# Attention's long steps before its short ones, and later tokens first through the output projection and the FFN, in a hybrid LRU / attention / RWKV-7 block

## The chip, the cores and the metric

The kernel runs on one core of a Trainium2 chip. The metric is device time of one execution in microseconds. Engines are named as in the profile: PE (TensorE, with PEld for its weight loads), DVE (VectorE), ACT (ScalarE), POOL (GpSimd), SP (SyncE, which issues nearly all transfers).

## The reference

One layer on 2048 tokens of width 1024, with 16 learned meta tokens in front (2064 rows). One input projection feeds three groups of heads; their outputs are concatenated to 1024 columns, projected, normalised and added; a gated FFN with a causal convolution of three taps follows.

```python
p = rms_norm(h, norm_mix_pre) @ w_in
oa = rg_lru_group(xa, ya, ...)                   # 256 columns, scan over tokens
ob = forgetting_attention_group(q, k, v, f, ...) # 512 columns, 8 heads of 64, causal
oc, _ = rwkv7_group(pc, ...)                     # 256 columns, scan over tokens
h = h + rms_norm(concat([oa, ob, oc]) @ w_out, norm_mix_post)
f = causal_dwconv(rms_norm(h, norm_ffn_pre) @ ffn_up, ffn_conv)   # 3 taps
gate, val = split(f)
h = h + rms_norm((gelu(gate) * val) @ ffn_down, norm_ffn_post)
# attention of one block of 128 queries, one head:
s = q @ k.T + (c[query] - c[key])   # c: running sum of log forget gates
o = softmax(where(key <= query, s, -inf)) @ v
```

Everything is float32. The kernel multiplies nearly all large products in three passes over high and low parts.

## The kernel before, in words

The framework plans the order of each engine's instructions itself, on a modelled timeline; what stands earlier in the program goes first where both could run. `tc.issue_after(ins)` puts what a block issues behind a given instruction on its engine. The stages, in the order of the program:

1. **Input projection** in three parts of the tokens (lines 158 to 281), with the recurrences beside it: `Beside.advance` (line 1842) steps the LRU blocks and the nine RWKV blocks (`Rwkv.block`, line 955) between column strips. The RWKV blocks follow each other through a state. Each has a triangular solve in which POOL (line 1101) and DVE (line 1102) take turns fifteen times. What is left of the recurrences when the projection ends is issued by `beside.finish()` (line 1958). The RWKV holds three PSUM banks (`ps_rw`, `ps_ae`), the projection five.
2. **Attention** (`Attn`, line 394). A step is one head and 512 queries, `b` of 0 to 3. It has `4b + 5` key tiles: 5 and 9 in a short step (b of 0, 1), 13 and 17 in a long one (b of 2, 3). `maxima` (line 485) multiplies queries with keys once to find each row's maximum; each piece goes to a PSUM bank (`mx`, line 448) that DVE reduces (line 512). `weights` (line 603) multiplies scores again (lines 635 and 636), takes exponentials on ACT (line 640), adds them up for the denominator, three of four on POOL and the rest on DVE (line 679), and multiplies with the values on PE (line 658). The maxima of a step are interleaved with the weights of the step two before it (`AHEAD`). After a step the denominator goes through DRAM and back (`total`, `invert`, `scale`), some ticks later. `run` (line 753) does the short steps of all eight heads, then the meta tokens, then the long steps. `mx` takes turns over two banks, or over three from the point `WIDE` on; the third one, `more`, is the RWKV's former `ps_ae`.
3. **Output projection** (`w_out_tile`, line 1421), 17 token tiles: tile 0 with two rows, tiles 1 to 16 with 128 rows each. A tile is 48 matmuls into two banks, then norm, residual and its row statistics. It reads 1024 rows of the concatenated heads (`scr["mix"]`), so it needs LRU, RWKV and all attention heads of its tokens. Its weights are loaded and split (line 144, 145) in memory that the RWKV gave back. Tiles 0 to 8 need only short attention steps, tiles 9 to 16 the long ones. Places 7 and 8 (`HELD`) are held behind the last but one attention step; from place 8 (`LATE`) on each tile is followed by an `ffn_norm` of the first FFN turn.
4. **FFN up** (`ffn_up`, line 1611) in three turns over the tokens (`SUPERS`), 684 tokens each, with 22 column pairs in each; the next turn's tokens are normalised by `between` during the one before.
5. **FFN down** (`Down`, line 1724) over pairs of token tiles, in two passes over the rows of `ffn_down`.

The order of the work around the change is written by hand in these few lines:

```python
for half, bs in enumerate(((0, 1), (2, 3))):   # 757
    if half: self.meta()
    for h in range(NH):
        self.wide = (half, h) >= WIDE          # 761, WIDE = (0, 5)
HELD = 7, 8                                    # 1821
for i, (f, rows) in enumerate(FFN_TILES):      # 1990
units = [(sup, j) for sup in range(SUPERS) for j in range(NFF)]   # 1618
```

Of the kernel before, what the change touches and what calls it, by code (L numbers as in the profile page):

```python
# [29 lines left out]
NFF = FF // P  # L30
# [363 lines left out]
class Attn:  # L394
# [358 lines left out]
    def run(self):  # L753


        ready = []
        for half, bs in enumerate(((0, 1), (2, 3))):
            if half:
                self.meta()
            for h in range(NH):  # L760
                self.wide = (half, h) >= WIDE
                keys = self.keys(h, 4 * bs[-1] + 5)
                for b in bs:
                    gen, total, out = self.maxima(h, b, keys), self.pieces(b), []

                    def fill(share, gen=gen, total=total, out=out):
                        while len(out) < min(total, share * total):
                            out.append(next(gen))

                    if len(ready) == self.AHEAD:  # L770
                        self.weights(*ready.pop(0), fill)
                    fill(1.0)
                    ready.append((h, b, keys, next(gen)))
        for step in ready:
            self.weights(*step, lambda share: None)
        self.flush()
        for _, _, f in self.later:
            f()
# [684 lines left out]
FFN_TILES = [(0, HALO)] + [(HALO + P * i, P) for i in range(SEQ // P)]  # L1463
# [3 lines left out]
SUPERS = 3  # L1467

# [33 lines left out]
def ffn_quarters(core, pool, sup):  # L1506

    t = pool.tile([P, len(QUARTERS), HK, FN], F32, tag="q", name=core.n("q"))
    q = {s: t[:, i] for i, s in enumerate(QUARTERS)}
    used = SEQ + HALO - FBLK * (2 * sup + 1)  # L1510
    if used < FN:
        for s in ("b0", "b1"):
            core.nc.gpsimd.memset(q[s][:, :, used:], 0.0)
    return q


def ffn_sums(core, q, after=nullcontext):

    q["t3"] = q["b0"]
    for k in range(HK):  # L1520
        for o, x, y in (("t1", "b0", "a0"), ("t2", "b1", "t1"), ("t3", "b1", "b0"), ("t4", "a1", "t2")):
            with after():
                core.nc.gpsimd.tensor_tensor(q[o][:, k], q[x][:, k], q[y][:, k], op=ALU.subtract)
            yield
# [86 lines left out]
def ffn_up(core, raws, ring, pool, banks, w_up, cw, scr, between, tokens):  # L1611

    nc = core.nc
    tt, stt = nc.vector.tensor_tensor, nc.vector.scalar_tensor_tensor
    turn = 0
    units = [(sup, j) for sup in range(SUPERS) for j in range(NFF)]
    ahead = UpWeights(core, raws, ring, w_up, scr, 0)
    ws = [ahead.operand(i) for i in range(7)]  # L1620
    xs = [tokens(0, i) for i in range(7)]

    def conv(src, u, j, n):
        y = pool.tile([P, FBLK], F32, tag="uy", name=core.n("uy"), bufs=UY)
        cc = u * NFF + j
        nc.scalar.activation(y[:, :n], src[:, 2 : n + 2], AF.Copy, scale=cw[:, 88 + cc : 89 + cc])  # L1626
        for i in (1, 0):
            stt(y[:, :n], src[:, i : n + i], cw[:, 44 * i + cc : 44 * i + cc + 1], y[:, :n], op0=ALU.mult, op1=ALU.add)  # L1628
        if u == 0:
            nc.scalar.activation(y[:, :n], y[:, :n], AF.Gelu_apprx_tanh)  # L1630
        return y

    def ending(g, v, j, b0, n):
        core.pooled = nc.gpsimd.tensor_tensor(v[:, :n], g[:, :n], v[:, :n], op=ALU.mult)  # L1634
        nc.sync.dma_start(scr["ff"][P * j : P * j + P, b0 : b0 + n], v[:, :n])

    for at, (sup, j) in enumerate(units):
        b0 = [FBLK * (2 * sup + i) for i in range(2)]
        n = [min(FBLK, SEQ - b) for b in b0]
        s = lambda tag: pool.tile([P, FN], F32, tag=tag, name=core.n(tag), bufs=1 if tag == "u2" else 2)[:]  # L1640
        between(sup, j)
        more = at + 1 < len(units)
        if more:
            ahead = UpWeights(core, raws, ring, w_up, scr, units[at + 1][1])
        ws_next, bank = [], {}
        turn ^= 1
        for i, (name, (_, _, at_)) in enumerate(PRODUCTS.items()):
            w, x = ws[i], xs[i]
            first = at_ not in bank
            if first:  # L1650
                bank[at_] = banks[turn].tile([P, 512], F32, tag="up", name=core.n("psu"))[:, :FN]
            ps = bank[at_]
            for k in range(HK):
                mm3(nc, ps, w[:, 0, k], w[:, 1, k], x[:, 0, k], x[:, 1, k], first and k == 0, k == HK - 1, not first)
            if j == NFF - 1 and more:
                xs[i] = tokens(sup + 1, i)
            if more:
                ws_next.append(ahead.operand(i))
            if name == "p1":
                ga = s("ga")  # L1660
                nc.scalar.activation(ga, ps, AF.Copy)
            elif name == "p5":
                vb = s("vb")
                nc.scalar.activation(vb, ps, AF.Copy)
            elif name == "p6":
                u2 = s("u2")
                nc.scalar.activation(u2, ps, AF.Copy)
            elif name == "p3":
                tt(ps, ps, u2, op=ALU.add)
                gb = conv(ps, 0, j, n[1])  # L1670
            elif name == "p7":
                tt(vb, ps, vb, op=ALU.add)
                vb = conv(vb, 1, j, n[1])
            elif name == "p2":
                tt(ps, ps, ga, op=ALU.add)
                ga = conv(ps, 0, j, n[0])
                ending(gb, vb, j, b0[1], n[1])
            else:
                va = conv(ps, 1, j, n[0])
                ending(ga, va, j, b0[0], n[0])  # L1680
        ws = ws_next
# [132 lines left out]
READY = 13  # L1814
PACE = 1.5

WIDE = (0, 5)

LATE = 8

HELD = 7, 8


class Beside:
# [54 lines left out]
def hybrid_block_kernel(ctx: ExitStack, tc: tile.TileContext, args, out):  # L1879
    a = {s: v[0] if s != "meta_tokens" else v for s, v in args.items()}  # L1880
    nc = tc.nc
    core = Core(tc, ctx)
    scr = scratch(tc, ctx, core)
# [4 lines left out]
    def run(gen):  # L1888
        for _ in gen:
            pass  # L1890
# [14 lines left out]
    with ExitStack() as p1:  # L1905
# [7 lines left out]
        with ExitStack() as p1a:  # L1913
# [5 lines left out]
            for part in range(3):  # L1919
# [6 lines left out]
                units = w_in_part(core, pools, ps_mm, a["w_in"], blocks, scr)  # L1926
# [42 lines left out]
    with ExitStack() as p3:  # L1969
# [11 lines left out]
        rs = {}  # L1981
        with p2:
            ps_wo.append(pool(p2, "ps_wo2", 1, space=PSUM, **right))
            banks = Banks(core, ps_wo)
            g_post = spread(pool(p2, "gpost", 1, **right), a["norm_mix_post"], "g_post")
            wp = pool(p2, "wp", 2, **right)
            w = w_out_load(core, wp, a["w_out"])
            todo = list(tiles[0])
            quarters = {0: ffn_quarters(core, qp, 0)}
            for i, (f, rows) in enumerate(FFN_TILES):  # L1990
                with tc.issue_after(at.steps[-2].ins) if i in HELD else nullcontext():
                    _, rs[i] = w_out_tile(
                        core, wp, banks, scr, w, x, meta, g_post, f + META - HALO, rows, rsv[:, 6 * i : 6 * i + 6]
                    )
                banks.wide = i >= LATE - 1
                if i >= LATE and todo:
                    q, f, rows = todo.pop(0)
                    ffn_norm(core, np_, ps_n, scr, f, rows, rs[q], g_fpre, quarters[0], 0)
                    if not todo:
                        run(ffn_sums(core, quarters[0]))  # L2000
        ps_f.append(pool(p3, "ps_f1", 3, space=PSUM, **early))
        uw += [pool(p3, "uw1", UWB, **early)] * UWB
        xo += [pool(p3, f"xo{i}", 1, **early) for i in range(3, XO)]
# [3 lines left out]

        def between(sup, j):

            sup += 1  # L2010
            if j == 1 and sup < SUPERS:
                quarters[sup] = ffn_quarters(core, qp, sup)
                todo[:] = tiles[sup]
            elif j == 1:
                kept = qp.tile([P, DOWN_KEPT, 2, 512], F32R, tag="q", name=core.n("qd"))
                down.extend(kept[:, i] for i in range(DOWN_KEPT))
            elif sup == SUPERS:
                if j == DOWN_FROM:
                    raw = lambda: tmp.tile([P, 512], F32, tag="uq", name=core.n("raw"))[:]
                    ws.append(down_operands(core, raw, lambda: down.pop(0), a["ffn_down"], scr, 0))  # L2020
            elif todo:
                q, f, rows = todo.pop(0)
                ffn_norm(core, np_, ps_n, scr, f, rows, rs[q], g_fpre, quarters[sup], sup)
                if not todo:
                    sums.append(ffn_sums(core, quarters[sup], lambda: tc.issue_after(core.pooled.ins)))
            else:
                for _ in range(2):
                    next(sums[-1], None)
# [78 lines left out]
```

## Time and profile before

| | us |
|---|---|
| median of 3 runs | 3129.16 (3125.92 to 3143.95) |
| the profiled execution | 3135.82 |
| its span in the profile, first to last instruction | 3134.1 |
| mean granted TensorE clock | 0.957 |
| PE busy | 2938.6 (94%) |
| DVE busy | 2218.7 (71%) |
| ACT busy | 1456.5 (46%) |
| POOL busy | 1320.1 (42%) |

A window is a stretch of the span in us from its start. Busy time is the union of an engine's instructions. PE's matmuls are pipelined and their ends are modelled, so 94% is not 94% of its peak. The granted clock is the share of full speed that TensorE had. A row of a view by line gives the count, the busy time, the mean duration in ns, and the idle time of the engine before those instructions with what ended it; a row of a view by window gives busy time and, in brackets, how many instructions fell into it.

### The profile page before, as it was taken

What the parts mean: (1) busy time and instruction counts of PE and PEld (TensorE: products, weight loads), DVE (VectorE), ACT (ScalarE), POOL (GpSimd) and SP (SyncE); (2) the same over time, 40 slices, a digit from 0 to 9 for tenths busy, and PEclk for the clock granted to TensorE, in tenths of its full rate; (3) what the DMA queues carried; (4) which work ended last, traced back from release to release, by engine and by line L of the source; (5) the groups of instructions that cost most, each with busy time, mean ns of one, the idle gap of its engine ahead of it and who ended that gap; (6) DMA issues with size and microseconds to landing.
All of it is one profiled execution on the core that took longest, in us unless ns stands there. A gap on an engine that the chain in (4) does not pass through costs nothing. (4 is left out here: it accounts for less than half of the span.)

```text
span 3134.1 us, 52572 instructions
## 1 busy us (share of the span) xinstructions
PE 2938.6 (94%) x18488; PEld 2504.0 (80%) x18488; DVE 2218.7 (71%) x4563; ACT 1456.5 (46%) x2716; POOL 1320.1 (42%) x1458
## 2 busy tenths in 40 slices
PE   6988899999988999999999899999999999999997
PEld 6978788888966665565557799999999999787776
DVE  6147665876678777877757787787778787647777
ACT  4133433444444434444543466666666665324332
POOL 3334334211013464645761235433533334547655
PEclk9989899999987888999999899999999999999999
DMA  6777766643453234535417365555555565435444
GB/s 195 224 237 224 219 197 217 204 129 109 116 128 83 72 84 108 147 96 134 97 43 232 123 188 168 165 172 167 165 166 165 168 189 163 170 105 165 148 155 141
DMA packets 493816, 484.10 MB, mean 154 GB/s; under 512 B 83200, under 2 KB 408010, under 8 KB 487904
## 3 DMA queue, kind: packets, MB, share of 16 engines
q1 hardware_dynamic: 493168, 480.36, 51.1%
q8 instruction: 145, 2.38, 0.3%
q14 instruction: 119, 0.97, 0.1%
q0 software_dynamic: 384, 0.39, 0.0%
HBM read 354.76 MB, written 125.87 MB: 153 GB/s over the span
## 5 line engine op out<-in xcount | busy, mean ns | idle before, releaser
L150 PE MATMUL psu<-xo,uw 128*128 128x344 f32 x1848 | 588.1, 323 | 7.8 <-DVE wx L1457 4.8
L151 PE MATMUL psu<-xo,uw 128*128 128x344 f32 x1848 | 593.2, 321 | 1.0 <-DVE xo L1529 1.0
L152 PE MATMUL psu<-xo,uw 128*128 128x344 f32 x1848 | 582.6, 320 | 0.0
L150 PE MATMUL psp<-xh,wh 128*128 128x384 f32 (+2 forms) x1152 | 384.5, 334 | 0.0
L152 PE MATMUL psp<-xh,wl 128*128 128x384 f32 (+2 forms) x1152 | 380.9, 331 | 2.4 <-DVE wl L145 2.4
L151 PE MATMUL psp<-xl,wh 128*128 128x384 f32 (+2 forms) x1152 | 381.7, 331 | 0.0
L150 PEld LDWEIGHTS psu<-xo,uw 128*128 128x128 f32 x1848 | 347.3, 189 | 9.3 <-DVE wx L1457 5.2
L151 PEld LDWEIGHTS psu<-xo,uw 128*128 128x128 f32 x1848 | 348.5, 189 | 1.3 <-DVE xo L1529 1.3
L152 PEld LDWEIGHTS psu<-xo,uw 128*128 128x128 f32 x1848 | 346.9, 189 | 0.0
L1528 ACT ACTIVATE uw<-uq 128x512 fp32r<-128x512 f32 x462 | 287.3, 627 | 104.4 <-PE psu L152 51.5
L1529 DVE TENSOR_TENSOR uw<-uq,uw 128x512 fp32r<-128x512 f32 x330 | 286.9, 874 | 62.8 <-ACT uw L1528 57.7
L640 ACT ACTIVATE p<-sc,bias 128x512 f32<-128x512 f32 (+4 forms) x352 | 197.7, 590 | 216.4 <-PE sc L636 182.1
L1529 POOL TENSOR_TENSOR uw<-uq,uw 128x512 fp32r<-128x512 f32 x132 | 181.4, 1374 | 255.9 <-ACT uw L1528 221.6
L1628 DVE SCALAR_TENSOR_TENSOR uy<-psu,ffn_cols,uy 128x342 f32<-128x342 f32 (+1 forms) x396 | 224.1, 568 | 90.1 <-ACT uy L1626 89.1
L1634 POOL TENSOR_TENSOR uy<-uy,uy 128x342 f32<-128x342 f32 (+1 forms) x132 | 136.6, 1035 | 323.0 <-DVE uy L1628 136.3
L679 POOL TENSOR_TENSOR acc<-acc,p 128x512 f32<-128x512 f32 (+3 forms) x208 | 229.4, 1105 | 91.3 <-ACT p L640 35.4
L152 PEld LDWEIGHTS psp<-xh,wl 128*128 128x128 f32 x1152 | 221.6, 192 | 9.7 <-issue 4.5
L150 PEld LDWEIGHTS psp<-xh,wh 128*128 128x128 f32 x1152 | 221.9, 193 | 8.4 <-issue 6.1
L151 PEld LDWEIGHTS psp<-xl,wh 128*128 128x128 f32 x1152 | 221.6, 192 | 6.5 <-issue 4.6
L1547 POOL TENSOR_TENSOR us<-us 128x512 f32<-128x512 f32 x88 | 131.9, 1499 | 218.2 <-DMA us<-in_ffn_up_dram 181.7
L512 DVE TENSOR_REDUCE mc<-mx 128x1 f32<-128x400 f32 (+5 forms) x320 | 172.2, 554 | 61.9 <-PE mx L509 57.3
L1529 DVE TENSOR_TENSOR fo<-u,fo 128x896 fp32r<-128x896 f32 x88 | 107.0, 1216 | 116.5 <-ACT fo L1528 116.5
(451 smaller groups left out, 6600.8 us busy)
## 6 DMA issues: line engine op xcount, KB each, us to landing
uq<-scr_us SPq DMA_DIRECT2D x264, 256.0 KB
uq<-in_ffn_up_dram SPq DMA_DIRECT2D x198, 256.0 KB
raw<-in_w_in_dram SPq DMA_DIRECT2D x72, 512.0 KB
us<-in_ffn_up_dram SPq DMA_DIRECT2D x44, 512.0 KB
scr_us<-us SPq DMA_DIRECT2D x22, 1024.0 KB
u<-scr_ff SPq DMA_DIRECT2D x88, 256.0 KB
scr_ff<-uy SPq DMA_DIRECT2D x110, 171.0 KB
q<-scr_qh SPq DMA_DIRECT2D x96, 128.0 KB
```

The costliest lines, as they stand in the source:

```text
L150: nc.tensor.matmul(out, ah, bh, start=first, stop=False, skip_group_check=more)
L151: nc.tensor.matmul(out, ah, bl, start=False, stop=False, skip_group_check=more)
L152: nc.tensor.matmul(out, al, bh, start=False, stop=last, skip_group_check=more)
L512: self.reduced = nc.vector.tensor_reduce(mc[:rows, i, ci : ci + 1], ps[:rows, :full], axis=AX.X, op=ALU.max)
L640: last = nc.scalar.activation(p[:rows, :w], ps[:rows, :w], AF.Exp, bias=bias[:rows, j : j + 1])
L679: eng.tensor_tensor(a, ps_[0][0][:rows, c0:n] if start and i == 1 else a, p[:rows, : n - c0], op=ALU.add)
L1528: core.nc.scalar.activation(hi, src, AF.Copy)
L1529: (eng or core.nc.vector).tensor_tensor(lo, src, hi, op=ALU.subtract)
L1547: add, sub = (lambda o, x, y, op=op: nc.gpsimd.tensor_tensor(o, x, y, op=op) for op in (ALU.add, ALU.subtract))
L1628: stt(y[:, :n], src[:, i : n + i], cw[:, 44 * i + cc : 44 * i + cc + 1], y[:, :n], op0=ALU.mult, op1=ALU.add)
L1634: core.pooled = nc.gpsimd.tensor_tensor(v[:, :n], g[:, :n], v[:, :n], op=ALU.mult)
```

## The change

The long steps of all heads come first and the short ones second; the third bank for maxima is used from the fifth head of the (now long) first half on. The output projection takes tiles 9 to 16 first and then 0 to 8, with places 6 and 7 held behind the last but one attention step. The FFN takes its turns in the order 2, 0, 1, so that its first turn needs tiles 11 to 16 (six tiles; turn 0 needs seven). No instruction's shape changes.

```diff
-        for half, bs in enumerate(((0, 1), (2, 3))):
+        for half, bs in enumerate(((2, 3), (0, 1))):
...
+ORDER = 2, 0, 1
...
-    units = [(sup, j) for sup in range(SUPERS) for j in range(NFF)]
+    units = [(sup, j) for sup in ORDER for j in range(NFF)]
-    xs = [tokens(0, i) for i in range(7)]
+    xs = [tokens(ORDER[0], i) for i in range(7)]
...
-                xs[i] = tokens(sup + 1, i)
+                xs[i] = tokens(units[at + 1][0], i)
...
-WIDE = (0, 5)
+WIDE = (0, 4)
+OUT_ORDER = [9, 10, 11, 12, 13, 14, 15, 16, 0, 1, 2, 3, 4, 5, 6, 7, 8]
-HELD = 7, 8
+HELD = 6, 7
...
-            todo = list(tiles[0])
-            quarters = {0: ffn_quarters(core, qp, 0)}
-            for i, (f, rows) in enumerate(FFN_TILES):
-                with tc.issue_after(at.steps[-2].ins) if i in HELD else nullcontext():
+            todo = list(tiles[ORDER[0]])
+            quarters = {ORDER[0]: ffn_quarters(core, qp, ORDER[0])}
+            for at_, i in enumerate(OUT_ORDER):
+                f, rows = FFN_TILES[i]
+                with tc.issue_after(at.steps[-2].ins) if at_ in HELD else nullcontext():
...
-                banks.wide = i >= LATE - 1
-                if i >= LATE and todo:
+                banks.wide = at_ >= LATE - 1
+                if at_ >= LATE and todo:
...
-            sup += 1
-            if j == 1 and sup < SUPERS:
+            turn = ORDER.index(sup) + 1
+            sup = ORDER[turn] if turn < SUPERS else None
+            if j == 1 and turn < SUPERS:
```

More of the change, by code (lines that the diff above doesn't have):

```diff
@@ L1994, in hybrid_block_kernel @@
                     )
-                banks.wide = i >= LATE - 1
-                if i >= LATE and todo:
+                banks.wide = at_ >= LATE - 1
+                if at_ >= LATE and todo:
                     q, f, rows = todo.pop(0)
-                    ffn_norm(core, np_, ps_n, scr, f, rows, rs[q], g_fpre, quarters[0], 0)
+                    ffn_norm(core, np_, ps_n, scr, f, rows, rs[q], g_fpre, quarters[ORDER[0]], ORDER[0])
                     if not todo:
-                        run(ffn_sums(core, quarters[0]))
+                        run(ffn_sums(core, quarters[ORDER[0]]))
         ps_f.append(pool(p3, "ps_f1", 3, space=PSUM, **early))
@@ L2016, in between @@
                 down.extend(kept[:, i] for i in range(DOWN_KEPT))
-            elif sup == SUPERS:
+            elif turn == SUPERS:
                 if j == DOWN_FROM:
```

## The prediction

> **What bounds the kernel now.** I read the page first, then the span cut by stage (in the table of windows), then counts of single lines in the same windows, then the waits.
>
> ```profile
> PE 2938.6 (94%) x18488; PEld 2504.0 (80%) x18488; DVE 2218.7 (71%) x4563; ACT 1456.5 (46%) x2716; POOL 1320.1 (42%) x1458
> PEclk9989899999987888999999899999999999999999
> ```
> TensorE is busy nearly everywhere, so a change can win only where its busy time is poor: where the clock row drops. The one long dip is slices 12 to 16 of 40. The windows are cut at the marks of the code: projection beside the RWKV, RWKV beside short attention steps, long steps beside the output projection, long steps alone, the rest of the output projection, FFN up, FFN down.
>
> ```profile
> core 0: us, PE busy (x) PEld busy (x) DVE busy (x) ACT busy (x) POOL busy (x), PEclk, DMA share, GB/s
> 548.00:862.00 314.00, 308.68 (x3055) 280.06 (x3055) 223.76 (x505) 141.64 (x261) 45.86 (x69) 1.00 0.47 140
> 905.00:1240.00 335.00, 299.72 (x2364) 200.90 (x2363) 260.70 (x811) 140.42 (x300) 150.17 (x236) 0.78 0.40 93
> 1240.00:1460.00 220.00, 205.66 (x883) 126.65 (x881) 171.49 (x404) 103.39 (x184) 116.55 (x121) 0.98 0.48 127
> 1460.00:1605.00 145.00, 135.70 (x581) 72.60 (x580) 109.00 (x249) 79.92 (x139) 114.20 (x128) 0.99 0.37 87
> 1605.00:1757.00 152.00, 136.99 (x622) 105.28 (x620) 100.59 (x263) 54.10 (x103) 37.85 (x37) 0.98 0.48 154
> 1757.00:2653.00 896.00, 890.09 (x5630) 888.48 (x5631) 692.87 (x1111) 562.37 (x1099) 358.97 (x310) 0.99 0.55 170
> 2653.00:3134.00 481.00, 446.30 (x1876) 354.64 (x1875) 324.72 (x496) 162.42 (x262) 283.49 (x360) 0.97 0.45 148
> ```
> I measure a stage by its yield: busy share of PE times granted clock. It is 0.98 in 548:862, 0.93 for long steps alone (135.70/145 x 0.99), 0.92 beside the output projection, 0.88 in 1605:1757, but 0.70 in 905:1240 (299.72/335 x 0.78). That stage holds 335 x 0.78 x 0.895 = 234 us of full-clock PE work in 335 us. The change reorders 905:1757, 852 us; the FFN stages keep their products and matmuls, and PE fills 890 of 896 us there, so I put them at no change.
>
> ```profile
> 905.00:1132.00 227.00, 28.29 (x70) 14.68 (x70) 0.75 0.40 93
> 1132.00:1213.00 81.00, 17.03 (x43) 8.39 (x43) 0.88 0.38 91
> 1240.00:1460.00 220.00, 39.90 (x105) 19.31 (x104) 0.98 0.48 127
> 1460.00:1605.00 145.00, 45.31 (x115) 21.06 (x115) 0.99 0.37 87
> ...
> 905.00:1240.00 335.00, 55.43 (x224) 19.86 (x224) 0.78 0.40 93
> 1460.00:1605.00 145.00, 51.15 (x224) 15.93 (x224) 0.99 0.37 87
> ...
> 905.00:1240.00 335.00, 64.22 (x145) 32.94 (x145) 0.78 0.40 93
> 1460.00:1605.00 145.00, 37.97 (x104) 19.23 (x103) 0.99 0.37 87
> ...
> 1240.00:1460.00 220.00, 87.39 (x336) 56.80 (x336) 16.34 (x25) 9.51 (x28) 0.98 0.48 127
> 1605.00:1757.00 152.00, 117.92 (x480) 89.88 (x480) 23.77 (x37) 13.60 (x40) 0.98 0.48 154
> ```
> These are the same windows for the score matmul of line 635 (one per key tile), the value matmul of line 658 (two per tile), the maxima of line 509, and the tile pswo of the output projection (48 matmuls a token tile). The short half has 8 x (5 + 9) = 112 key tiles, the long half 8 x (13 + 17) = 240. So all short steps run in 905:1213, 113 scores, beside the RWKV, and 7 output tiles (336/48) beside long heads 0 to 3; 10 more (480/48) come at the end.
>
> **The change, part by part.**
>
> *Prices.* Long steps alone: 115 scores, 112 value tiles and 104 maxima are 110 tiles' work in 135.70 x 0.99 = 134 us of full clock, 1.22 us a tile. A short tile is narrower (338 columns on average against 431, by the widths in the loop): 0.96 us. The RWKV stage then holds 112 x 0.96 = 107 us of short steps, some 16 us of the first long steps (7 scores, 33 maxima), and the rest of its 234, 111 us, is RWKV. An output tile beside attention: (205.66 x 0.98 - 105 x 1.22) / 7 = 10.5 us.
>
> *Long steps beside the RWKV* (line 757). Work 111 + 240 x 1.22 = 404 us, now in one stage. Its yield is the unknown. From below: the present 0.70. From above: 0.93, long steps by themselves; RWKV beside the dense 384-column products of the projection even had 0.98, with the clock at 1.00. I take 0.88, nearer to the upper rows, since the stage gets what those two have and the present one lacks: wide matmuls that don't run out before the RWKV does. 404/0.88 = 459 us, so the last long step ends near 1364 (1341 at 0.93).
>
> ```profile
> PE sc L635 <- DMA q<-scr_qh: 6.6, 1, 6.6
> PE eps L1014 <- DVE rwix L77: 4.6, 1, 4.6
> PE mx L509 <- DVE q L538: 3.3, 3, 2.6
> ...
> L1101 POOL TENSOR_TENSOR rwitmp<-rwix,rwia x135: 230/431/1469, 296.9 to 1143.7; 128x16 f32<-128x16 f32 x8, 128x24 f32<-128x24 f32 x8, 128x32 f32<-128x32 f32 x8, 128x40 f32<-128x40 f32 x8
> L1034 PE MATMUL eps<-rwsq,bones x36: 218/379/793, 270.6 to 1100.7; 128*128 128x256 f32 x32, 128*128 128x64 f32 x4
> L1270 PE MATMUL rps<-rwsg,g_up x36: 218/379/792, 479.9 to 1233.7; 128*128 128x256 f32 x32, 128*128 128x64 f32 x4
> L144 ACT ACTIVATE woh<-raw x8: 1043/1057/1059, 1246.3 to 1277.3; 128x1024 fp32r<-128x1024 f32 x8
> ```
> The first three rows are TensorE's longest waits in 905:1240; no engine holds it for long, it is slowed by its clock. [...]
>
> What the long steps delay: the solve's products on POOL (135 in nine blocks, line 1101; three blocks solve in this stage, 45) each go back and forth with VectorE, and POOL will hold more running sums (114.20 of 145 us busy in the long stretch against 150.17 of 335 now). At one sum's length of some 1.1 us (92.27 us for 81, the row of line 679 below) each, that is up to 50 us: the RWKV would end near 1284 instead of 1234 (line 1270 is its last product). The long steps cover it until 1364. Without that cover the output weights are late next: their load, 8 pairs of splits, begins only when the RWKV's memory is free and ends at 1278 now, 45 us after the RWKV; 1284 + 45 = 1329 still fits, barely. Long keys and values (twice as many columns) are read beside the RWKV now, through the same SP queue with the same number of issues a head and step; the DMA share there is 0.40, so nothing.
>
> *Third bank from the fifth long head* (WIDE). It is the RWKV's scratch bank, last written at 1100.7; the fifth long head comes at about half of 459 us, near 1130. Nothing waits; without it maxima have two banks, as beside the projection now. 0, at most a few us either way.
>
> *Short steps beside the output projection* (OUT_ORDER, HELD). PE work: 107 + 6 x 10.5 = 170 us, at 0.92 it is 185 us. But short steps are rich in VectorE work:
>
> ```profile
> 905.00:1240.00 335.00, 10.63 (x23) 70.38 (x71) 0.78 0.40 93
> 1460.00:1605.00 145.00, 19.24 (x26) 92.27 (x81) 0.99 0.37 87
> ...
> L512 DVE TENSOR_REDUCE mc<-mx 128x1 f32<-128x400 f32 (+7 forms) x126 | 62.0, 499 | 14.3 <-PE mx L509 10.3 <-DMA rwia<-da 2.5 <-PE sc L636 0.7
> L515 DVE CUSTOM_DVE_ANT_0 mj<-mx,future 128x128 f32<-128x128 f32 x72 | 19.4, 274 | 4.1 <-PE mx L509 4.1
> L538 DVE TENSOR_TENSOR q<-mx,ident 4x512 fp32r<-4x512 f32 x17 | 11.6, 682 | 2.8 <-PE mx L527 2.4
> L718 DVE TENSOR_TENSOR o<-o,rb 64x512 f32<-64x512 f32 x13 | 10.0, 796 | 0.0
> L695 DVE TENSOR_TENSOR o<-po,oh 64x400 f32<-64x400 f32 (+1 forms) x16 | 9.9, 617 | 2.8 <-DMA scr_mix<-o 1.3 <-ACT o L694 0.9 <-ACT oh L692 0.4
> ...
> L1456 DVE SCALAR_TENSOR_TENSOR pswo<-pswo,rs,g_post 128x512 f32<-128x512 f32 x15 | 10.7, 754 | 0.3
> L1457 DVE TENSOR_TENSOR wx<-wx,pswo 128x512 f32<-128x512 f32 x14 | 9.0, 678 | 0.0
> L88 DVE SCALAR_TENSOR_TENSOR rs<-rs 128x1 f32<-128x1 f32 x24 | 7.4, 309 | 0.6
> L145 DVE TENSOR_TENSOR ml<-raw,mh 128x1024 fp32r<-128x1024 f32 x6 | 7.3, 1221 | 0.1
> ```
> (The two rows on top are the sums of line 679, DVE then POOL; the second group is of VectorE in 905:1240, the third of its last 100 us before FFN.) A short step has on average 7 reductions of 0.499, 4 diagonal ones of 0.274, the two of 0.682 and 0.796, 0.617, and 7/4 sums of 10.63/23: 7.5 us, about 8 with small ones. An output tile: 2 x 0.754, 2 x 0.678, 1.221 and 12 small ones near 0.3: about 8. So 16 x 8 + 6 x 8 = 176 us; VectorE was never over 0.78 busy in these stages (260.70/335, 171.49/220), which makes 226 us. I take the middle of 185 and 226, 206 us: short steps end at 1570. Another row agrees: where the RWKV thins out, 43 tiles ran in 81 us, 1.88 us each, 211 us for 112.
>
> *The rest of the output projection.* Before: 10 tiles and 15 key tiles in 152 us, so (152 - 15 x 1.22)/10 = 13.4 us a tile. Six instead of seven tiles run ahead, so 11 are left (two of them held for the end of attention as before): 147 us, to 1717 against 1757. The first FFN turn needs six norm tiles instead of seven and two clears of 4 columns on POOL; both lie under three last output tiles. Turns 2, 0, 1 leave the FFN's work as it is; the down projection starts with tokens of turn 0, written some 300 us earlier. 0.
>
> *Sum.* 459 + 206 + 147 = 812 us instead of 852: 40 us less. The profiled execution took 3135.82 us, 1.72 beside its span of 3134.1, and lies 6.7 us over the median 3129.16. The same 40 us off the median gives 3089 us. About 1% (31 us) is what a measurement of this kernel can tell from no change.
>
> **Rivals.**
>
> *The RWKV holds the clock down itself.* If its many small matmuls and not the lack of wide ones make 0.78, the first 335 us yield some 0.75 again: 251 of the 404 us, and the other 153 at 0.93 take 165 us: 500 us, +41. Total +1: 3130 us. For: the dip lasts as long as the RWKV runs without projection. Against: 548:862 has the RWKV too, at 1.00.
>
> *The change doesn't do what it says.* The order of instructions puts the RWKV first, and long steps get no more out of its gaps than short ones: 123 us of their work in 335, then (293 - 123)/0.93 = 183 us. 518 us, total +19: 3148 us. For: attention comes after the RWKV in the program. Against: long steps have fewer chains per column and two steps' scores ready.
>
> *Slower: short steps keep their own pace.* If the chain of each short step (maxima, shift, scores, exponential, sums, two steps ahead) and not the RWKV's share sets 905:1213, 16 steps take 308 us again, with the output tiles hidden in them: 102 us over my 206, 62 in total, 3191 us. It decides from 246 us for the stage on, 15.4 us a step. For: 19 us a step now, and two of the three long waits above are such links. Against: the 43 tiles in 81 us, 13 us for a step of 7.
>
> **How the numbers follow.** The forecast has 0.57 (its own range 3045 to 3117: a yield of 0.93 and 185 us at one end, 0.83 in the first stage at the other), the clock rival 0.15, the one without effect 0.09, the slower one 0.19. Of the forecast's share four fifths are below 3098: faster 0.45. The rest of the forecast and the first two rivals are within 1%: 0.36; the third is slower: 0.19. The range reaches from the forecast's own low end, less 5 us for the third bank, 3040, to 3175, short of the slower rival's full price, and so leaves out some 2 in 10.
>
> **What would show it.** Right: granted clock above 0.9 over the RWKV's last third, over 150 scores by its end, last long step before 1400, short steps under 15 us each, first FFN product near 1717. Wrong: a clock of 0.8 there, an RWKV that ends after 1340 with the output tiles behind it, or more than 246 us from the last long to the last short step.

## The result, and the profile after

The changed kernel takes 3167.63 us (median of 4 runs, 3160.55 to 3176.48) against 3135.95 for the kernel before, measured beside it (4 runs, 3125.92 to 3143.95): a ratio of 1.0118 [1.0085, 1.0152]. It is slower by about 1%, some 32 us, where 40 us less were predicted. Its profiled execution took 3166.99 us with a span of 3165.3.

First the page's busy times and its clock row, then the span cut by stage. The stages end at the RWKV's last product, the last long step, the last short step and the first product of the FFN.

```profile
PE 2944.3 (93%) x18488; PEld 2505.4 (79%) x18488; DVE 2213.8 (70%) x4563; ACT 1456.4 (46%) x2716; POOL 1305.7 (41%) x1458
PEclk9989899999987989999989999999999999999999
```
```profile
core 0: us, PE busy (x) PEld busy (x) DVE busy (x) ACT busy (x) POOL busy (x), PEclk, DMA share, GB/s
905.00:1245.00 340.00, 291.53 (x2326) 192.36 (x2325) 255.70 (x687) 136.71 (x270) 148.28 (x188) 0.83 0.31 68
1245.00:1427.00 182.00, 159.46 (x682) 82.30 (x680) 125.47 (x304) 93.05 (x157) 122.85 (x140) 0.93 0.50 125
1427.00:1644.00 217.00, 201.94 (x914) 132.24 (x912) 154.92 (x471) 104.53 (x213) 117.92 (x175) 0.96 0.45 122
1644.00:1787.00 143.00, 124.49 (x541) 94.63 (x540) 101.61 (x273) 44.93 (x86) 20.16 (x20) 0.95 0.48 159
1787.00:2686.00 899.00, 893.75 (x5639) 891.39 (x5640) 695.84 (x1113) 560.94 (x1100) 356.59 (x309) 0.99 0.56 170
2686.00:3165.00 479.00, 446.42 (x1875) 355.45 (x1874) 323.17 (x496) 162.44 (x261) 283.26 (x359) 0.97 0.46 149
```
Total busy time of PE is where it was (2944.3 against 2938.6), the FFN stages are too (899 and 479 us against 896 and 481). Nearly all of the loss lies in 905 to 1787: 882 us instead of 852. (The 1605 at which the prediction cut the kernel before lies ahead of the end of its last attention step, near 1649; so the stages of the two kernels do not match one by one.) Yield by yield, as the prediction read it: the RWKV stage has 291.53/340 x 0.83 = 0.71 where it had 0.70; its clock rose from 0.78 to 0.83, and PE's busy share fell from 0.895 to 0.857. Long steps alone have 159.46/182 x 0.93 = 0.81 where they had 0.93. The counts of scores (line 635), of output products (tile pswo) and the last RWKV and first FFN products say how far each stage got:

```profile
905.00:1245.00 340.00, 50.41 (x122) 24.19 (x122) 0.83 0.31 68
1245.00:1335.00 90.00, 23.90 (x59) 11.10 (x58) 0.91 0.56 145
1335.00:1427.00 92.00, 26.71 (x65) 11.83 (x65) 0.96 0.44 106
...
1427.00:1644.00 217.00, 86.27 (x336) 61.55 (x336) 16.40 (x24) 9.60 (x28) 0.96 0.45 122
1644.00:1787.00 143.00, 117.64 (x480) 88.31 (x480) 26.64 (x41) 13.61 (x40) 0.95 0.48 159
...
L1270 PE MATMUL rps<-rwsg,g_up x36: 217/380/793, 477.1 to 1244.6; 128*128 128x256 f32 x32, 128*128 128x64 f32 x4
...
L150 PE MATMUL psu<-xo,uw x1848: 313/321/652, 1788.8 to 2685.8; 128*128 128x344 f32 x185
```
122 long scores fit beside the RWKV, not many more than before, when 114 stood ahead of the RWKV's last product (all but two of them short). The other 124 scores (118 long and six short) took 182 us. The prediction asked for over 150 scores by the RWKV's end.

The waits of all engines in the stretch of long steps alone, changed kernel, then the kernel before in its own stretch of long steps alone (1460 to 1605):

```profile
ACT p L640 <- POOL acc L679: 26.0, 16, 5.6
POOL acc L679 <- DVE acc L679: 19.4, 13, 2.8
PE sc L635 <- ACT p L640: 16.8, 13, 5.5
POOL acc L679 <- DMA scr_den<-acc: 15.9, 4, 5.6
...
POOL acc L679 <- DVE acc L679: 12.8, 10, 2.2
...
PE sc L635 <- ACT p L640: 4.8, 11, 1.4
...
POOL acc L679 <- DMA scr_den<-acc: 2.3, 3, 1.7
...
ACT p L640 <- POOL acc L679: 1.9, 3, 1.3
```
Columns: us in all, times, longest. The waits form a chain that was much shorter before. VectorE's quarter of the running sums is late (19.4, before 12.8), and the buffer of a sum is not free until its transfer has left (15.9, before 2.3). So POOL's sums are late and with them the buffers of exponentials, for which ACT waits (26.0, before 1.9). So PE waits for exponentials before it has a bank for the next scores (16.8, before 4.8).

### The profile page after: what moved, and what is told of

The parts are those of the page before. It is cut to its first block, busy times and chain, and to the rows that moved or that the text cites. A ratio compares the mean times of both kernels' runs of the same rounds, so it can differ in the third digit from the quotient of the medians.

```text
span 3165.3 us, 52534 instructions
## 1 busy us (share of the span) xinstructions
PE 2944.3 (93%) x18488; PEld 2505.4 (79%) x18488; DVE 2213.8 (70%) x4563; ACT 1456.4 (46%) x2716; POOL 1305.7 (41%) x1458
## 5 line engine op out<-in xcount | busy, mean ns | idle before, releaser
L1531 POOL TENSOR_TENSOR uw<-uq,uw 128x512 fp32r<-128x512 f32 x132 | 180.1, 1364 | 289.3 <-ACT uw L1530 260.2
L512 DVE TENSOR_REDUCE mc<-mx 128x1 f32<-128x512 f32 (+3 forms) x320 | 172.8, 554 | 65.2 <-PE mx L509 63.4
L1530 ACT ACTIVATE fo<-u 128x896 fp32r<-128x896 f32 x88 | 81.2, 922 | 233.5 <-POOL u L1746 123.2
```

The source lines that it names most:

```text
L512: self.reduced = nc.vector.tensor_reduce(mc[:rows, i, ci : ci + 1], ps[:rows, :full], axis=AX.X, op=ALU.max)
L1530: core.nc.scalar.activation(hi, src, AF.Copy)
L1531: (eng or core.nc.vector).tensor_tensor(lo, src, hi, op=ALU.subtract)
```

## Experiments

Each kernel ran beside the kernel before on the same chip. "Against before" is the difference of the two medians. The kernel before had medians of 3126.33 to 3135.95 us on the chips used, so two kernels from different chips compare to some 5 to 10 us.

### How much the overlap with the RWKV is worth, in each order

**e1_wait_after.** The changed kernel with attention's matmuls behind the RWKV's last one:

```diff
-            nc.tensor.matmul(                        # 1270
+            self.tail = nc.tensor.matmul(
...
-            at.run()
+            with tc.issue_after(R.tail.ins):
+                at.run()
```


> The changed kernel, with all of attention's matmuls put behind the last RWKV matmul in TensorE's order. Theory (the RWKV's own chain sets its stage, attention only takes slots the order gives it): the RWKV still ends near 1200, against 1245 beside the long steps; attention's 126 tiles that were beside it come after, at 1.3 us each, 164 us, so the total is some +110 to +130 us. Rival (the two compete for TensorE and VectorE, so the RWKV alone is much shorter): it ends near 1100 and the total is +20 to +40 us.

Measured: 3252.85 us, 1.0385 [1.034, 1.043], 85 us over the change, between the two sides; the RWKV ended at 1150.

**e5_wait_before.** The same edit in the kernel before.

> The kernel before, with all of attention's matmuls put behind the last RWKV matmul in TensorE's order; the counterpart of the run that did this to the changed kernel (3252.85 us). With nothing beside the RWKV in either, the two differ only in what goes beside the output projection. Theory (the 30 us are lost after the RWKV: long steps without a partner, then short steps with the output tiles): 3205 to 3225 us, the difference of 30 us or more remains. Rival (they are lost beside the RWKV, where short steps fill better than long ones): 3240 to 3260 us, the difference is gone.

Measured: 3244.87 us, 1.0368 [1.0339, 1.0396], 112 us over the kernel before, and the difference between the two orders is gone, as the rival has it. Windows of e1 (RWKV alone, long heads 0 to 3, long heads 4 to 7, short steps with seven output tiles, the rest), then of e5 (RWKV alone, short steps alone, long steps with output tiles):

```profile
905.00:1150.00 245.00, 175.24 (x1714) 143.01 (x1713) 131.06 (x397) 58.61 (x130) 33.77 (x62) 0.53 0.21 46
1150.00:1348.00 198.00, 164.62 (x636) 87.43 (x635) 130.17 (x306) 89.83 (x149) 112.70 (x126) 0.88 0.37 90
1348.00:1510.00 162.00, 149.77 (x666) 79.83 (x664) 115.07 (x286) 83.87 (x145) 119.62 (x134) 0.96 0.44 101
1510.00:1727.00 217.00, 199.14 (x938) 133.84 (x934) 148.58 (x482) 106.10 (x217) 122.05 (x182) 0.98 0.48 127
1727.00:1872.00 145.00, 126.09 (x538) 96.09 (x538) 102.37 (x271) 44.86 (x86) 20.13 (x20) 0.94 0.48 156
...
905.00:1140.00 235.00, 170.46 (x1676) 137.91 (x1675) 127.46 (x389) 57.65 (x127) 31.61 (x61) 0.54 0.20 45
1140.00:1333.00 193.00, 155.62 (x640) 88.44 (x640) 135.65 (x390) 87.28 (x170) 109.38 (x169) 0.81 0.48 121
1333.00:1755.00 422.00, 395.34 (x1701) 236.10 (x1701) 297.81 (x738) 197.88 (x355) 247.83 (x271) 0.98 0.39 96
```
This is the clearest result. With nothing beside the RWKV the two orders differ by 8 us, 1.0385 against 1.0368, which is not told apart from none: the order of halves as such costs next to nothing. With the overlap they differ by some 32. So the loss is that long steps gain less from running beside the RWKV than short ones, 85 us against 112.

The rows say how: the RWKV alone lasts 235 to 245 us. With attention woven in it ends after 340 us (122 long scores) or 329 (114, all but two of them short): 95 us more either way. What is then missing behind it is 360 - 182 = 178 us of long steps, 1.5 us a tile at the pace of long steps alone (360/240); in the old order all the short steps are gone, 193 us alone, 1.7 us a tile (193/112), with 0.81 of the clock. So the overlap saves 178 - 95 = 83 us of long steps, but 193 - 94 = 99 us of short ones; the rest of the 112 lies behind (from the end of the short steps on, e5 takes 1909 us where the kernel before takes 1900 from the RWKV's end). The RWKV's gaps hold about as many tiles of either kind, and a short tile alone is the dearer one.

### Edits that turned out to cost nothing

**e2_ffn012.** The change with `ORDER = 0, 1, 2`.

> The changed kernel with the FFN's turns in the old order 0, 1, 2 (long steps first and tiles 9 to 16 first stay). Theory (the loss lies in attention): within 8 us of the changed kernel; a few us slower, because the first turn's tiles come out last and seven norm tiles stand behind the last output tiles. Rival (later tokens first costs the 30 us): back near the time before, some 30 us faster.

Measured: 3167.01 us, 1.0106 [1.006, 1.0153]: the order of FFN turns is free. The run also shows how far a single stage time can be trusted: with the same 121 scores ahead of it, the RWKV's last product (line 1270) came at 1257.4 us here and at 1244.6 in the change.

**e4_held7.** The change with `HELD = (7,)`.

> The changed kernel with only place 7 of the output projection held behind the last but one attention step, HELD = (7,), so that a seventh tile may run among the short steps. Theory: -5 to +5 us, since short steps and output tiles are limited together. Rival (the end loses for want of a tile beside the short steps): -10 us or more.

Measured: 3164.41 us, 1.0104 [1.0066, 1.0142]: 3 us less, not told apart from none.

### The third bank for maxima

**e3_wide_late.** The change with `WIDE = (1, 0)`, so that the long steps have two banks throughout.

> The changed kernel with the third bank for maxima only from the short half on, WIDE = (1, 0). Theory (the long steps without the RWKV are held by the running sums on POOL and the buffers of exponentials that wait for them, not by maxima): 0 to +8 us. Rival (the third bank pays in the long heads 4 to 7): +15 us or more.

Measured: 3195.72 us, 1.0183 [1.0129, 1.0237], 28 us over the change and as far over e2 on the same chip; its runs spread over 20 us (3181.85 to 3202.24). That is the rival's price. The bank that the prediction had at "0, at most a few us" is worth some 28 us.

**e8_wide3.** The change with `WIDE = (0, 3)`, a head earlier.

> The changed kernel with the third bank one head earlier, WIDE = (0, 3). The bank is last written by the RWKV near 1125 us, and the fourth head's maxima begin near 1149. Theory (banks): -3 to -10 us, a quarter of what the bank brought for four heads (28 us). Rival (the bank helps only where nothing runs beside): 0 or slower.

Measured: 3146.23 us, 1.006 [1.0038, 1.0081], 21 us under the change and the nearest of all versions to the kernel before with all its work. Scores in the RWKV stage and in the long steps alone:

```profile
905.00:1263.00 358.00, 55.40 (x136) 26.56 (x136) 0.84 0.33 73
1263.00:1406.00 143.00, 41.21 (x105) 19.25 (x104) 0.96 0.53 130
```
14 more tiles came in beside the RWKV, which ended 18 us later, and the rest ran at 143/105 = 1.36 us a tile instead of 182/124 = 1.47. That is more than twice what was expected of one head more.

**e11_wide2.** `WIDE = (0, 2)`, two heads earlier.

> The changed kernel with WIDE = (0, 2), the third bank two heads earlier than in the change. In the order of instructions 121 scores stand ahead of the last RWKV product, as in the change; with WIDE = (0, 3) 135 do. Theory (each head with the bank is worth some 7 us or more): 3126 to 3141 us, 5 to 20 us under the run with (0, 3). Rival (the bank is the RWKV's scratch until 1128 us, and the third head's maxima begin near 1089, so they wait for it): 5 to 20 us over it.

Measured: 3166.38 us, 1.0114 [1.0083, 1.0145]: the gain of e8 is gone again. That is the rival's price, but its trace shows no wait of TensorE's maxima for the RWKV above 0.8 us. PE's static order has 121 scores ahead of the RWKV's last product here, 135 in e8, 121 in the change and 114 in the kernel before. Among these three new ones the time goes with that count, but e16 below has 134 and gains nothing, so the count alone does not set the time.

**e9_wait_after_bank.** e1 with `WIDE = (0, 0)`: no RWKV beside, three banks from the start.

> The changed kernel with attention behind the RWKV (3252.85 us), and the third bank for maxima in use from the first long head on, WIDE = (0, 0). Theory (long steps want three banks; the change leaves half of their heads with two): 3208 to 3223 us, 30 to 45 us less, heads 0 to 3 at 1.35 us a tile as heads 4 to 7 instead of 1.63. With that it lies under the counterpart in the old order (3244.87 us). Rival (long steps alone are held by the running sums and VectorE, banks or not): 3242 us or more.

Measured: 3254.86 us, 1.0393 [1.0359, 1.0428], 2 us over e1, where 30 to 45 less had been expected. With no RWKV beside, long steps gain nothing measurable from the third bank.

**e10_before_two_banks.** The kernel before with `WIDE = (2, 0)`, never a third bank.

> The kernel before with two banks for maxima throughout, WIDE = (2, 0). Theory (its long steps live on the third bank too): 35 to 60 us slower than before, so that the old order with two banks is no better than the new one. Rival (beside the output projection and with short steps first the bank is worth little): at most 10 us slower.

Measured: 3200.78 us, 1.0226 [1.0183, 1.0268], 69 us, more than either side gave it. Waits of its long steps (1260 to 1670):

```profile
ACT p L640 <- POOL acc L679: 61.1, 37, 5.9
DVE acc L679 <- POOL acc L679: 60.5, 25, 7.4
POOL acc L679 <- DMA scr_den<-acc: 60.3, 8, 17.8
```
The same chain as in the change, and longer: a sum waits up to 17.8 us for the transfer of the sum two steps before it. The bank is not all that differs: the order has 106 scores ahead of the RWKV's last product here, not 114.

### What holds the long steps: VectorE, sums, buffers

**e6_reduce64.** The change with each piece of maxima reduced over its first 64 columns only:

```diff
-  self.reduced = nc.vector.tensor_reduce(mc[...], ps[:rows, :full], ...)            # 512
+  self.reduced = nc.vector.tensor_reduce(mc[...], ps[:rows, : min(full, 64)], ...)
```


> The changed kernel, with each maximum of line 512 taken over the first 64 columns of its piece only (the rest of the piece is left out of the maximum), so that VectorE loses some 0.35 us for each of 320 pieces and TensorE nothing. Theory (two banks of maxima wait for VectorE's reductions, beside the RWKV and after it): -40 us or more, all of it before the output projection's end; the long heads without the RWKV near 1.2 us a tile. Rival (the running sums on POOL set the pace of the long steps): -15 us at most.

Measured: 3118.48 us, 0.9956 [0.994, 0.9973], 49 us under the change.

**e12_before_reduce64.** The same edit in the kernel before.

> The kernel before with each maximum of line 512 taken over the first 64 columns of its piece only; control to the same edit in the changed kernel (49 us less there). Theory (maxima weigh more in the new order, where they have two banks for longer): 15 to 35 us less than before. Rival (VectorE's time weighs the same in both orders): 45 to 55 us less.

Measured: 3129.36 us, 0.9996 [0.9971, 1.0021]: 3 us. The groups of line 512 in the change and in e6, then e6's windows (RWKV, long steps alone, short steps, rest):

```profile
L512 DVE TENSOR_REDUCE mc<-mx 128x1 f32<-128x512 f32 (+3 forms) x320 | 172.8, 554 | 65.2 <-PE mx L509 63.4 <-PE sc L636 0.4
...
L512 DVE TENSOR_REDUCE mc<-mx 128x1 f32<-128x64 f32 x320 | 65.0, 214 | 90.9 <-PE mx L509 89.1 <-PE sc L636 0.2
...
905.00:1234.00 329.00, 283.20 (x2360) 182.26 (x2359) 223.49 (x709) 139.88 (x276) 154.78 (x195) 0.89 0.35 76
1234.00:1394.00 160.00, 143.21 (x641) 78.89 (x641) 87.84 (x287) 87.41 (x147) 120.05 (x128) 0.96 0.53 129
1394.00:1598.00 204.00, 194.17 (x922) 132.43 (x924) 140.40 (x466) 106.11 (x216) 122.08 (x179) 0.98 0.49 132
1598.00:1738.00 140.00, 123.00 (x548) 93.32 (x544) 98.72 (x276) 44.36 (x86) 19.61 (x20) 0.96 0.50 163
```
The same VectorE work (108 us; 107 in the kernel before) costs 49 us in the new order and 3 in the old. With it gone from both, the new order is no longer the slower one: 3118.48 us against 3129.36, 0.9956 against 0.9996, each against the kernel before on its own chip. By the profiles the gain lies in the first three stages: 11, 22 and 13 us, 3 in the rest, where the 11 are within the scatter that e2 shows. (The order of instructions differs a little too: 124 scores ahead of the RWKV's last product, 121 in the change.) In the long steps alone ACT no longer waits for a sum:

```profile
ACT p L640 <- PE sc L636: 50.3, 45, 4.5
DVE mc L512 <- PE mx L509: 45.4, 30, 6.8
...
DVE acc L679 <- POOL acc L679: 10.4, 7, 2.0
...
POOL acc L679 <- ACT p L640: 9.7, 7, 3.0
```
What is left of ACT's waits for exponentials is for TensorE's products. So the chain shown above hangs on the time that VectorE spends on maxima, though VectorE was busy only 125.47/182 = 0.69 of the stretch and 0.75 of the RWKV stage.

**e18_share8.** `SHARE = 8`: one running sum in eight on VectorE instead of one in four, the others on POOL.

> The changed kernel with one running sum in eight on VectorE instead of one in four, the rest on POOL. Theory (VectorE, late with maxima, is what the long steps lack): 5 to 25 us less. Rival (POOL with its sums is what they lack): 10 us or more slower.

Measured: 3153.75 us, 1.008 [1.0052, 1.0109]: 14 us under the change, 10 under e17 on the same chip. That is near the limit of what can be told, with the same 121 scores ahead of the RWKV's last product. It speaks for VectorE and not POOL as the engine in want, since POOL gets the work, at some 1.1 us a sum where VectorE takes 0.74 in the prediction's rows.

**e7_fewer_sums.** The change without the running sums of key tiles 2 to 4b - 1, on both engines:

```diff
+                if 1 < j < 4 * b:
+                    continue
```


> The changed kernel without the running sums of key tiles 2 to 4b-1 of each step (left out of the denominator): 10 of 16 sums in a step of 17 tiles, 6 of 12 in one of 13, 2 of 8 in one of 9. Theory (maxima and their banks): -15 us at most. Rival (POOL's sums and the exponentials' buffers that wait for them): -30 us or more, with the waits of ACT for POOL gone.

Measured: 3132.25 us, 1.0005 [0.9987, 1.0024], 35 us under the change, the price of the rival; ACT's waits for POOL's sums are gone. It fits the chain, but doesn't tell its two engines apart, since a quarter of the sums dropped are VectorE's.

**e16_total_in_score_bank.** The denominator's products in a bank of the scores (`ps = self.ps("sc", 2)`, line 704) instead of one of the maxima.

> The changed kernel with the total of a step's denominators (line 704) in one of the two score banks instead of a maxima bank. Theory (the total waits behind maxima for a bank): 8 to 25 us less. Rival (score banks are as scarce, or the total isn't late for want of a bank but for VectorE's sums): 0 or slower.

Measured: 3174.24 us, 1.0123 [1.0094, 1.0152]: no gain, though 134 scores stood ahead of the RWKV's last product. So it is not shown that the denominator holds up the maxima's banks; the banks of the scores may be as scarce, which this run can't tell apart.

**e13_acc3, e14_acc3_w3, e15_before_acc3.** A third buffer for the sums (`self.t([P, 512], "acc", bufs=3)`, line 653) in the change, in e8 and in the kernel before.

> The changed kernel with three buffers for the running sum instead of two. Theory (the sum of a step goes through a maxima bank to DRAM before its buffer is free; with maxima late the buffer is late, POOL waits 16 us for it in 1245:1420 against 4 us before, the exponentials pile up behind it, and ACT and the scores wait): 12 to 30 us less, 3138 to 3156 us, POOL's waits for that transfer gone. Rival (the late maxima themselves hold the scores): 5 us less at most.

> The changed kernel with three buffers for the running sum and the third bank one head earlier, WIDE = (0, 3). If the two causes are one chain (bank, then sum buffer): 3130 to 3142 us, little under the run with the bank alone (3146 us). If they are two: 3115 to 3130 us, under the kernel before.

> The kernel before with three buffers for the running sum; control. Theory: 0 to 5 us less, since POOL waits for the buffer only 4 us in its long steps. Rival (the buffer is a general limit): 12 us less or more.

Measured: 3241.9 us, 1.0339 [1.0311, 1.0367]; 3247.84, 1.0364 [1.0336, 1.0392]; 3253.55, 1.0381 [1.0354, 1.0408]. These answer another question than they were asked. Scores of e13:

```profile
905.00:1145.00 240.00, 0.00 (x0) 0.00 (x0) 0.52 0.12 28
1145.00:1350.00 205.00, 52.86 (x126) 24.38 (x126) 0.88 0.50 112
```
Not one score ran beside the RWKV: with the added buffer attention began only behind it, and the three kernels are like e1 and e5. That it was for lack of memory is a guess, which e17 fits. Without the overlap the buffer makes 11 us less than e1 in the changed kernel and 9 more than e5 in the one before, both on other chips and near the limit of what can be told.

**e17_acc3_o3.** The third buffer for sums, with one of the four buffers of `o` (line 690) given up for it.

> The changed kernel with three buffers for the running sum and, to make room in the memory, three instead of four for the output of a step, so that attention still runs beside the RWKV (117 scores stand ahead of the last RWKV product, 121 in the change). Theory (the sum's buffer is the link through which late maxima hold the long steps): 8 to 25 us less than the change, with POOL's wait for the transfer of the sum below 5 us in the long heads. Rival (the buffer is a symptom): -5 us to slower.

Measured: 3164.16 us, 1.0106 [1.0072, 1.0139], 3 us under the change. Now attention starts in time. But the total hides two opposite effects. The stages of e17 (long steps alone, then short steps) and a wait of its short steps:

```profile
1229.00:1405.00 176.00, 159.07 (x705) 83.70 (x704) 126.97 (x306) 95.57 (x165) 130.31 (x151) 0.96 0.53 130
1405.00:1641.00 236.00, 205.90 (x912) 136.57 (x911) 154.34 (x476) 104.48 (x211) 110.79 (x168) 0.92 0.42 113
...
ACT o L694 <- DMA scr_mix<-o: 14.4, 4, 6.3
```
The last long step ended at 1405 instead of 1427, and there POOL's wait for the transfer and ACT's wait for POOL's sums are gone from the trace; the long steps alone ran at 176/129 = 1.36 us a tile instead of 1.47. (Of the 22 us, 16 lie in the RWKV stage, where e2 shows a scatter of 13.) The short steps then took 236 us instead of 217, and ACT waited for the buffer of `o` to be written out, a wait that the change does not show in its short steps. So the run trades one buffer for another. Whether the sum's buffer is a cause of the loss in the long steps or a mark of the congestion, it does not settle; its trace of the long steps speaks for a cause.

No version beat the kernel before with all its work in place; e6, which is under it, does part of the maxima.

## Why the prediction was wrong

**The step that failed** is "I take 0.88", the yield of long steps beside the RWKV, "nearer to the upper rows". The work was sized well: 390 us of full clock by the rows (291.53 x 0.83 + 159.46 x 0.93) against 404. But 390 us took 522, a yield of 0.75, where 459 had been forecast: 63 us. The reason that was given, "wide matmuls that don't run out before the RWKV does", held for the clock only in part, 0.83 instead of 0.78, and not for the yield, since PE was less often busy. In the RWKV's last third (1132 to 1245) the clock was 0.86, between the 0.9 that was to show the forecast right and the 0.8 that was to show it wrong. The last long step ended at 1427, not near 1364, and the first FFN product came at 1789, not near 1717.

What the runs show in place of 0.88 is this. The overlap with the RWKV is worth 85 us to long steps and 112 to short ones (e1, e5), and VectorE's maxima hold the long steps back through sums and buffers. With that work cut by 108 us in all, the two stages take 329 + 160 = 489 us instead of 522 (e6), a yield of 0.80 (283.20 x 0.89 + 143.21 x 0.96 over 489). So this cut gives back 33 of the 63 us; why the yield is then 0.80 and not 0.88 stays open.

It went as the rival "The change doesn't do what it says" has it, with 9% of the chances: "long steps get no more out of its gaps than short ones". Its 518 us for the stage stand against 522, and its +19 in all against +30 in these stages. The kernel's order of instructions and e1 with e5 bear it out: 95 us more RWKV stage for 114 or 122 tiles. That its total came so close is partly luck. It put the rest behind the RWKV at a yield of 0.93, and it came at 0.81; but it also had 170 us of work there, and there were 148 (159.46 x 0.93).

**The second failed term** is the third bank, "0, at most a few us either way": 28 us for four heads (e3), another 21 for one more (e8), 69 in the old order (e10), where e8 and e10 change the order of instructions too. "Nothing waits" was read from when the bank is free, and not from what two banks cost the maxima. That a third bank lets maxima run further ahead while VectorE is late fits the waits, but no run singles it out.

**A blind spot in the working** stands behind both. VectorE was counted for short steps beside the output projection; for long steps beside the RWKV only TensorE's yield was asked for. VectorE had 0.78 in the RWKV stage before as well. Since e6 takes 49 us from the change and e12 3 from the kernel before, the price of the same VectorE work depends on the order. A reason can be argued: before, the first long heads ran beside output products, with PE busy 211.53 of 226 us at 0.98 of the clock, so that VectorE's delays had other matmuls to hide under. The two stages of the kernel before, with the RWKV and behind it:

```profile
905.00:1234.00 329.00, 293.85 (x2337) 197.72 (x2336) 255.13 (x797) 136.15 (x294) 146.94 (x233) 0.78 0.39 93
1234.00:1460.00 226.00, 211.53 (x908) 129.83 (x908) 177.05 (x419) 107.66 (x191) 119.78 (x124) 0.98 0.48 127
```
The trace of e12, one execution, shows that this is not the whole reason. There the RWKV's last product came at 1203.6 us instead of 1233.7, with the same 114 scores ahead of it, so VectorE's maxima cost time beside the RWKV in the old order too. But the last score of attention came at 1633 instead of 1643: two thirds of the gain were lost again in the long steps, 429 us instead of 409, with a granted clock of 0.95 instead of 0.99. Why the clock was lower, no run here shows.

**Right in size were** the short steps beside the output projection (217 us measured, 206 forecast, 13.6 us a step; not the 308 of the slower rival) and the rest of the output projection (143, 147 forecast). The first is partly luck: seven output tiles lie in that stage (336/48) and not six, TensorE's work was 194 us of full clock (201.94 x 0.96) and not 170, at a yield of 0.89, and VectorE was 0.71 busy and not 0.78. Right were also the RWKV's end (1245, where up to 1284 was allowed for) and the costs of nothing for the FFN's order (e2) and `HELD` (e4). The rival "The RWKV holds the clock down itself" was half right: alone the RWKV has a clock of 0.53 (e1), and the stage kept a low one; but its 3130 us came from a rest at 0.93.

**What stays open.** How the 32 us divide between the order of instructions in the RWKV stage and VectorE behind it: e8 and e11 move both at once, and e16 has e8's count of scores without its gain. Whether a third buffer for sums pays where nothing is given up for it (e17). Why the third bank gains nothing behind the RWKV (e9) and 21 to 69 us elsewhere. And why long steps alone have 1.36 to 1.65 us a tile in the new order, where they had 145/115 = 1.26 before.

## What to carry to other kernels

Price a stage that gets new work by the demand on each engine, and not by the busy share and clock of the one that binds now: the engine that was slack beside one partner can bind beside another, even at 0.69 busy, when its delays run through buffers to the one that counts. Work that fills gaps is to be counted in slots that the order of instructions gives it; here the kind of step that is dearer by itself gained more from them. A run of each order with the overlap taken away (e1, e5) shows in two runs whether the order or the overlap is at stake.

## What was not expected of the hardware

The RWKV alone runs at close to half clock, though PE is not idle: 175.24 of 245 us busy at 0.53 (e1). TensorE's longest waits in that stretch:

```profile
PE rps L1266 <- DVE rww L1259: 25.9, 4, 9.5
PE rps L1209 <- DVE rwst L1213: 7.2, 9, 1.8
PE eps L1363 <- DVE rwe L1361: 6.8, 1, 6.8
PE rps L1058 <- DVE rwsc L1063: 5.2, 1, 5.2
```
These four rows come to 45.1 of the 245 us. The RWKV alone has much the same clock in other runs: 0.54 in e5 (905 to 1140), 0.53 in e9 (905 to 1151) and 0.52 in e13 (905 to 1145). What holds the clock down there, no run here shows.

The second surprise is how sharply a buffer can act: one more 128x512 buffer cost 74 us (e13) because an overlap was lost. With another buffer given up for it the total moved by 3 us, but the long steps ended 22 us earlier and the short ones took 19 us more (e17).
